# Moving the first branch into the last head of a delta rule: a hybrid decoder layer on one core

## The chip, the core and the metric

The kernel runs on one core of a Trainium2 chip. The metric is the device time of one execution in microseconds (us). The core has a tensor engine (PE, with its weight loads shown as PEld), a vector engine (DVE), a scalar engine (ACT), GpSimd (POOL) and SyncE (SP), which issues nearly all DMAs of this kernel. Each engine takes its instructions in the order in which the program lists them.

## The reference, cut to what matters

One decoder layer on 1024 tokens of width 1024, in float32: a half-weighted SwiGLU block, a mixer of two branches, a second SwiGLU block, and a final norm. The mixer:

```python
qa, ka, va, qkv_b, beta_raw, decay_raw, gdn_gate, gate_a, gate_b = jnp.split(h @ w_in, offsets, axis=-1)
# branch A: three groups of dilated windows, 4 heads of 64 each
for gi, (window, dilation) in enumerate(DSW_GROUPS):
    o, lse = dilated_window_attention(qa[:, :, sl], ka[:, :, sl], va[:, :, sl], window, dilation)
    outs.append(o)
    lses.append(lse)
wts = jax.nn.softmax(jnp.stack(lses, axis=0), axis=0)
ya = jnp.einsum('gbsh,gbshd->bshd', wts, jnp.stack(outs, axis=0))
# branch B: gated delta rule, 8 heads of 128
S_t = exp(g_t) * S_{t-1} (I - beta_t k_t k_t^T) + beta_t v_t k_t^T;  o_t = S_t q_t / sqrt(Dk)
ob = rmsnorm(ob, gdn_out_norm) * jax.nn.silu(gdn_gate)
merged = sigmoid(gate_a) * (ya @ w_branch_a) + sigmoid(gate_b) * (yb @ w_branch_b)
return merged @ w_out
```

## The kernel before, in words

**Arithmetic.** A float32 product is made of three matmuls of a reduced float32 type: each operand is split into a high part (a copy on ACT) and a low part (a subtraction on DVE). `split_to` (L165) does it for data, `ff_split` (L208) for weights, into rings of nine tiles `fH` and `fL`. A "wide" matmul streams 512 columns; the transposes and the delta rule's own products are "narrow" ones.

**Stages.** First SwiGLU with its down projection, attention of three groups (`attention_pair`), eight heads of the delta rule (`mixer`, L1260), the merge of the branches (`merge_out`, L1325), second SwiGLU with its down projection (`Down`, `ff_down`). The down projection is seven products of 11 pairs each, four PSUM banks at a time; with `outer=LAST` (4) the last product works its last four pairs bank by bank, so that each bank of a row can be finished while the others are still summed.

**The heads.** For each head, `gdn_keys` makes keys and queries with a short convolution (L950), the decay (L1001) and the matrices; `gdn_inverse` inverts a triangular matrix by 31 dependent steps on DVE (L1040 to L1046) and four groups of narrow matmuls (L1074 to L1096); `gdn_values` adds the values; `gdn_scan` (L1176) walks eight chunks: per chunk the narrow products L1191, L1195, L1199, L1204, L1211 with a DVE or ACT operation between each two. Head h+1 is prepared while head h is scanned. Between these narrow steps PE works on wide projections, among them 16 gate tiles (`gate_tile`), of which the last are kept for the last head.

**Combination of the groups.** `combine` (L903) loads, for each of eight row tiles, the three groups' outputs and maxima, forms their softmax weights (an exponential at L917, small DVE operations), the weighted sum (L926 to L929), two transposes (L932) and a store to the buffer `yad`. All eight tiles stand in head 0.

**The merge.** `merge_out` opens its own pool of on-chip memory, loads `yad` (L1336), splits it (`yaH`, `yaL`), multiplies it by `w_branch_a` in 96 wide matmuls and copies the results into `x2` (L1351). It loads the eight heads' results `ybd` and splits each into `hH` and `hL` (L1353 to L1355). Then come the second branch's products, the sigmoid gates (L1367) and the output product.

**What sets the order.** The program is traced once; a planner (`arrange`) takes it as a graph, gives every operation a price and a rank (the longest priced way to the end) and lists, engine by engine, the operation of highest rank that is ready; the program is then built a second time in that order. So one edit can move instructions far from it. Buffers' rings are fixed by the order of the source.

Of the kernel before, what the change touches and what calls it, by code (L numbers as in the profile page):

```python
# [15 lines left out]
P = 128  # L16
# [473 lines left out]
class Down:  # L490

    def __init__(self, C, wd):
        self.C = C
        self.wd = wd.rearrange("(p o k) n -> o k p n", o=2, k=P)
        self.lefts = {}
        self.raws = {}
        self.home = {}
        self.quarters = {}
        self.ops = []

    def left(self, n, p, tag="e"):
        if (n, p) not in self.lefts:
# [69 lines left out]
    def operands(self, n, p):  # L572
        C = self.C
        v = self.left(n, p)
        h = C.wp.tile([P, 512], F32R, name="fH", tag="fH", bufs=9)
        C.nc.scalar.copy(h, v.bitcast(F32))  # L576
        C.nc.vector.tensor_tensor(out=v, in0=v.bitcast(F32), in1=h.bitcast(F32), op=ALU.subtract)  # L577
        return (h, v), self.right(n, p)
# [29 lines left out]
def ff_down(C, x_dram, D_, done, mid=None):  # L608

    nc = C.nc  # L610
    acc = [None] * NT

    def part(t, n):
        if acc[t] is None:
            acc[t] = row(C, C.fx, "acc", None, None)
        return acc[t][:, n * 512:n * 512 + 512]

    def add(out, ps, base):
        nc.vector.scalar_tensor_tensor(out, ps, 0.5, base, op0=ALU.mult, op1=ALU.add)

    def e1(j, ps):
        nc.scalar.mul(part(j, 1), ps, 0.5)

    def e2(j, ps):
        add(part(j, 0), ps, part(j, 1))

    def e6(j, ps):
        add(part(j, 1), ps, part(j, 1))

    def e7(j, ps):  # L630
        add(part(4 + j, 0), ps, part(j, 1))

    def e5(j, ps):
        add(part(4 + j, 1), ps, part(4 + j, 0))
        add(part(j, 1), ps, part(j, 1))

    def residual(t):
        xt = row(C, C.fx, "xt", None, None)
        nc.sync.dma_start(xt, x_dram[t * P:t * P + P])
        nc.vector.tensor_tensor(out=acc[t], in0=acc[t], in1=xt, op=ALU.add)  # L640

    def e3(j, ps):
        add(part(j, 1), ps, part(j, 1))
# [12 lines left out]
    def side(p):
        if p < NT:
            residual(p)
        D_.last_sums(p)

    D_.product(0, e1, side=homes)
    D_.product(1, e2)
    D_.product(2, e6)
    D_.product(3, e7)
    D_.product(4, e5)
    D_.product(5, e3, side=side)
    D_.product(6, e4, LAST, mid)


def consts(C, I):  # L670
# [229 lines left out]
            nc.sync.dma_start(dst, o)  # L900


def combine(C):  # L903

    nc = C.nc
    for t in range(NT):
        oc = C.ms.tile([P, 792], F32, name="oc", tag="xs", bufs=2).rearrange("p (g q f) -> p g q f", g=3, q=2)
        for g in range(3):
            nc.sync.dma_start(oc[:, g], C.od[g][t * P:t * P + P])
# [266 lines left out]
def gdn_scan(C, X):  # L1176
# [6 lines left out]
    with band(C, f"h{h}"):  # L1183
# [45 lines left out]
        for q in range(2):  # L1229
# [2 lines left out]
                nc.tensor.transpose(ps[:, c * P:c * P + P], o[:, q * 4 + c, :], C.ident)  # L1232
            sl = slice(q * 512, q * 512 + 512)
            nc.vector.scalar_tensor_tensor(X.g[:, sl], ps, C.gon, X.g[:, sl], op0=ALU.mult, op1=ALU.mult)
        nc.sync.dma_start(C.ybd[h], X.g)


def gdn_consts(C, I):
# [21 lines left out]
def mixer(C, tc, I):  # L1260
# [9 lines left out]
    def fill(n):  # L1270
        for _ in range(n):
            if gates:
                gate_tile(C, w_in, *gates.pop(0))
# [8 lines left out]
    with tc.tile_pool(name="mx", bufs=1, reuse_waits="tile") as C.mx:  # L1282
# [17 lines left out]
                    n += 1  # L1300
        with tc.tile_pool(name="gd", bufs=1, reuse_waits="tile") as C.gd:
            X = gdn_keys(C, w_in, 0, decay(0))
            with band(C, "att"):
                combine(C)
            gdn_inverse(C, X)
            gdn_values(C, w_in, X)
            for h in range(HEADS):
                Y = None
                if h < HEADS - 1:
                    Y = gdn_keys(C, w_in, h + 1, decay(h + 1, FILL[1][h]))  # L1310
                gdn_gate(C, w_in, X)
                if h == HEADS - 1:
                    fill(len(gates))
                gdn_scan(C, X)
                if Y is not None:
                    gdn_inverse(C, Y)
                    gdn_values(C, w_in, Y)
                X = Y
# [6 lines left out]
def merge_out(C, tc, I, gB2):  # L1325
# [4 lines left out]
    def load(name):  # L1330
        return C.fx.tile([P, T], F32, name=name, tag="ld", bufs=2)

    ya = {}
    for a in (0, 1):
        v = load("yal").rearrange("p (k t) -> p k t", k=2)
        nc.sync.dma_start(v, C.yad[:, :, a * 512:a * 512 + 512])  # L1336
        for k in range(2):
            ya[k, a] = ff_e(C, "yaH", F32R), ff_e(C, "yaL", F32R)
            split_to(C, *ya[k, a], v[:, k])
    x2 = [row(C, C.fx, "x2", None, None) for _ in range(NT)]  # L1340

    def branch_a(f, a):
        return x2[a * 4 + f // 2][:, f % 2 * 512:f % 2 * 512 + 512]

    for f in range(8):
        if f % 4 == 0:
            W = load_w(C, (lambda r: r[:, :T].rearrange("p (k n) -> p k n", k=2),
                           I["w_branch_a"][:, f * P:f * P + 512].rearrange("(k p) n -> p k n", p=P)))
        for a in (0, 1):
            pa = proj(C, lambda k: [v[:, f % 4 * P:f % 4 * P + P] for v in W[k]], a, "tC" if a else "mm", 2, [ya[0, a], ya[1, a]])  # L1350
            nc.scalar.copy(branch_a(f, a), pa)  # L1351
        yb = row(C, C.fx, "ybl", None, None)
        nc.sync.dma_start(yb, C.ybd[f])  # L1353
        for ts in (slice(0, 512), slice(512, 1024)):
            split_to(C, C.hH[:, f, ts], C.hL[:, f, ts], yb[:, ts])  # L1355
    del ya, v, yb, W
    for a in (0, 1):
        ts = slice(a * 512, a * 512 + 512)
        m = []
        for f in range(8):  # L1360
# [5 lines left out]
            nc.sync.dma_start(sg[:, 1], C.sgbd[f][:, ts])  # L1366
            nc.scalar.activation(sg, sg, AF.Sigmoid)  # L1367
            pb = proj(C, lambda k: [v[:, k % 4 * P:k % 4 * P + P] for v in halves[k // 4]], a, "tC" if f % 2 else "mm")
            nc.vector.tensor_tensor(out=sg[:, 0], in0=sg[:, 0], in1=branch_a(f, a), op=ALU.mult)
            nc.vector.tensor_tensor(out=sg[:, 1], in0=sg[:, 1], in1=pb, op=ALU.mult)  # L1370
            nc.vector.tensor_tensor(out=sg[:, 0], in0=sg[:, 0], in1=sg[:, 1], op=ALU.add)
            m.append((ff_e(C, "mH", F32R), ff_e(C, "mL", F32R, "s3" if f > 4 else "e")))
# [33 lines left out]
def open_pools(C, tc, st):  # L1406
# [25 lines left out]
def layer(tc, I, out):  # L1432
# [6 lines left out]
    with ExitStack() as st:  # L1439
# [84 lines left out]
class Program:  # L1524
# [149 lines left out]
    def cost(self, k):  # L1674
# [13 lines left out]
            n *= c  # L1688
        q = self.queue[k]
        if q == 0:  # L1690
            t = {"R": n / 2.4 + 13, "T": 109, "F": 223, "S": n * 0.83 + 106, "s": n * 0.83 + 106, "Q": 117 if n > 32 else 63}[self.kind[k]]
            return t, t + 190
        ps = any(self.place[a["memref"]][0] == "PSUM" for a in aps)
        if q == 1:
# [191 lines left out]
```

## Time and profile before

| what | value |
|---|---|
| time, median of 3 runs (lowest to highest) | 2556.34 us (2556.09 to 2561.18) |
| the profiled execution | 2554.51 us |
| its span, first to last instruction | 2552.8 us |
| mean granted clock of PE | 0.994 |
| DVE, ACT busy | 1766.6, 974.1 us |

The span holds: the first SwiGLU with its projections to about 700 us, the attention to about 990, the heads to about 1690, the merge and the second SwiGLU after that. In the rows of a timeline the columns are start, duration (us), engine, line, operation, output <- inputs, shapes and a count; in brackets stands the idle time of the engine before it, and what ended it. In the rows of groups, the busy time and the mean length in ns stand behind the count, then the idle time ahead of the group.

### The profile page before, as it was taken

The numbers are of one execution on the slowest core, as the hardware profiler recorded it, in microseconds if no ns is written. First come the engines' busy times: TensorE is split into PE (matmuls) and PEld (weight loads), VectorE is DVE, ScalarE is ACT, GpSimd is POOL, SyncE is SP. The second block draws the span as 40 slices with busy tenths as digits, with TensorE's granted clock in tenths as the row PEclk, the third lists the DMA queues.
The fourth block names the chain that finished last, engine by engine and source line by source line (L and its number), as shares of the span: only waits on it lengthen the run. The fifth ranks groups of instructions, "written<-read, shape, count | busy, mean of one in ns | idle before, by whom it ended". The sixth has DMA issues, their size and how long they took to land.

```text
span 2552.8 us, 34782 instructions
## 1 busy us (share of the span) xinstructions
PE 2490.4 (98%) x12739; PEld 2070.5 (81%) x12739; DVE 1766.6 (69%) x4035; ACT 974.1 (38%) x1875; POOL 24.6 (1%) x36
## 2 busy tenths in 40 slices
PE   7999999999999999899999999989999999999997
PEld 7888888888988888678887887868888888888886
DVE  7866666768744455988878778345768666667588
ACT  4432232444423345542444334154443332223444
POOL 0000000000000000000000000000000000000000
PEclk9999999999999999999999999999999999999999
DMA  4233224836253322322121122165542223238453
GB/s 162 84 107 119 94 101 169 288 112 219 96 138 92 92 82 80 95 57 56 55 67 53 54 57 80 55 202 189 193 138 83 92 98 120 91 118 303 137 170 119
DMA packets 257786, 301.04 MB, mean 118 GB/s; under 512 B 41456, under 2 KB 174800, under 8 KB 257616
## 3 DMA queue, kind: packets, MB, share of 16 engines
q1 hardware_dynamic: 255312, 292.53, 34.8%
q10 hardware_dynamic: 2304, 6.29, 1.1%
q8 instruction: 100, 1.64, 0.3%
q14 instruction: 70, 0.57, 0.1%
HBM read 217.34 MB, written 75.14 MB: 115 GB/s over the span
## 4 chain that ended last, share of the span: by engine, by line
PE 86%; DVE 9%; DMA 2%; ACT 1%; issue 1%; SPq 0%; DVEq 0%; ACTq 0%
PE mm L161 19%; PE tC L404 13%; PE mm L404 9%; PE tM L404 8%; PE mm L584 5%; PE tC L584 4%; PE tM L584 4%; PE tA L584 4%; PE tA L161 3%; PE mm L697 2%; PE mm L274 2%; PE tC L274 2%; PE mm L1387 2%; PE tC L1387 1%; PE tC L161 1%; PE tA L890 1%
## 5 line engine op out<-in xcount | busy, mean ns | idle before, releaser
L216 ACT CAST fH<-fraw 128x512 fp32r<-128x512 f32 x482 | 290.2, 619 | 597.8 <-PE tC L404 258.8
L217 DVE TENSOR_TENSOR fL<-fraw,fH 128x512 fp32r<-128x512 f32 x482 | 318.9, 685 | 158.9 <-ACT fH L216 142.7
L161 PE MATMUL mm<-hH,fH 128*128 128x512 f32 x896 | 359.3, 403 | 2.3 <-ACT xp L828 2.3
L161 PE MATMUL mm<-hL,fH 128*128 128x512 f32 x896 | 356.0, 398 | 0.0
L161 PE MATMUL mm<-hH,fL 128*128 128x512 f32 x896 | 353.9, 399 | 0.1
L161 PEld LDWEIGHTS mm<-hH,fH 128*128 128x128 f32 x896 | 169.1, 189 | 33.7 <-ACT xp L828 2.7
L161 PEld LDWEIGHTS mm<-hH,fL 128*128 128x128 f32 x896 | 168.9, 188 | 33.6 <-issue 1.0
L161 PEld LDWEIGHTS mm<-hL,fH 128*128 128x128 f32 x896 | 169.1, 189 | 29.9 <-issue 0.3
L404 PE MATMUL mm<-hH,fH 128*128 128x512 f32 x320 | 124.5, 389 | 0.0
L404 PE MATMUL mm<-hH,fL 128*128 128x512 f32 x320 | 123.7, 389 | 0.0
L404 PE MATMUL mm<-hL,fH 128*128 128x512 f32 x320 | 122.6, 389 | 0.0
L577 DVE TENSOR_TENSOR hid<-hid,fH 128x512 fp32r<-128x512 f32 x154 | 104.5, 684 | 9.9 <-ACT fH L576 9.9
L576 ACT CAST fH<-hid 128x512 fp32r<-128x512 f32 x154 | 94.9, 616 | 14.4 <-DMA hid<-hd1x 9.1
L969 DVE SCALAR_TENSOR_TENSOR ka<-xp,cw,ka 128x512 f32<-128x512 f32 x96 | 73.9, 781 | 19.6 <-ACT ka L967 19.0
L216 ACT CAST fH<-hH 128x512 fp32r<-128x512 f32 x68 | 42.3, 622 | 86.8 <-PE tC L584 36.0
L431 DVE TENSOR_TENSOR e<-tC,e 128x512 f32<-128x512 f32 x40 | 27.3, 686 | 66.9 <-PE tC L404 66.9
L404 PEld LDWEIGHTS mm<-hH,fL 128*128 128x128 f32 x320 | 60.1, 188 | 12.5
L404 PEld LDWEIGHTS mm<-hL,fH 128*128 128x128 f32 x320 | 60.1, 188 | 12.5
L404 PEld LDWEIGHTS mm<-hH,fH 128*128 128x128 f32 x320 | 60.1, 188 | 12.5
L584 PE MATMUL tC<-fH 128*128 128x512 f32 x176 | 68.6, 390 | 0.0
L584 PE MATMUL tC<-fL,fH 128*128 128x512 f32 x176 | 68.5, 389 | 0.0
L584 PE MATMUL mm<-fL,fH 128*128 128x512 f32 x176 | 68.4, 390 | 0.0
(402 smaller groups left out, 6111.3 us busy)
## 6 DMA issues: line engine op xcount, KB each, us to landing
fraw<-in_w_in_dram SPq DMA_DIRECT2D x66, 512.0 KB, 3.7
fraw<-in_ffn_w_gate_dram SPq DMA_DIRECT2D x22, 1024.0 KB, 5.2
fraw<-in_ffn_w_up_dram SPq DMA_DIRECT2D x22, 1024.0 KB, 7.3
hL<-in_ffn_w_down_dram SPq DMA_DIRECT2D x8, 1024.0 KB, 6.9
fraw<-in_ffn_w_down_dram SPq DMA_DIRECT2D x8, 1024.0 KB, 5.7
fraw<-in_w_branch_b_dram SPq DMA_DIRECT2D x8, 1024.0 KB, 5.1
fraw<-in_w_out_dram SPq DMA_DIRECT2D x8, 1024.0 KB, 5.3
vb<-xp ACTq DMA_DIRECT2D x48, 128.0 KB, 2.4
```

The lines of the kernel that those rows point to most:

```text
L161: nc.tensor.matmul(ps, w, x, start=k == 0 and i == 0, stop=k == kt - 1 and i == 2)
L216: nc.scalar.copy(h, src)
L217: nc.vector.tensor_tensor(out=l, in0=src, in1=h.bitcast(F32), op=ALU.subtract)
L274: nc.tensor.matmul(ps[:, n0:n0 + n], w, x[:, k, c], start=k == 0 and i == 0, stop=k == KT - 1 and i == 2)
L404: nc.tensor.matmul(ps, w, x, start=opens and k == 0 and q == 0, stop=k == 3 and q == 2, skip_group_check=True)
L431: tt(out=p1[i], in0=ps, in1=p1[i], op=ALU.add)
L576: C.nc.scalar.copy(h, v.bitcast(F32))
L577: C.nc.vector.tensor_tensor(out=v, in0=v.bitcast(F32), in1=h.bitcast(F32), op=ALU.subtract)
L584: self.C.nc.tensor.matmul(ps, x[:, m], w, start=p == 0 and i == 0, stop=p == NPAIR - 1 and i == 2)
L697: nc.tensor.matmul(ps[:, :n], h[:, k, b * P:b * P + P], W[k][w], start=k == 0 and i == 0, stop=k == KT - 1 and i == 2)
L969: nc.vector.scalar_tensor_tensor(o, x, w, o, op0=ALU.mult, op1=ALU.add)
L1387: nc.tensor.matmul(ps, mx[:, c], W[k][w], start=i == 0, stop=i == len(seq) - 1)
```

## The change

1. `combine` takes a list of tiles and is called after each head's scan: two tiles with heads 1 and 6, one with heads 2 to 5, none with head 0.
2. The first branch is computed by a new function `branch_a` in the last head, ahead of its scan: loads of `yad`, splits, 96 matmuls, copies, and eight stores to new buffers `pad`. It also loads the results of heads 0 to 6 and splits them into `hH`, `hL` (`keep_head`). The last head's result is split where it is made and not stored.
3. `merge_out` loads the first branch's product from `pad` into `x2` and starts with the second branch.
4. In the second down projection the last product works its last seven pairs bank by bank (`closing`), and the high parts of its last five pairs lie in the ring `hid`.
5. The planner's price for the narrowest matmuls (32 columns) goes from 63 to 32.

```diff
@@ Down.operands
+        if self.closing and n == 4 and p >= NPAIR - 5:
+            h = ff_e(C, "hid", F32R)
+        else:
+            h = C.wp.tile([P, 512], F32R, name="fH", tag="fH", bufs=9)
@@ ff_down
-    D_.product(6, e4, LAST, mid)
+    D_.product(6, e4, D_.closing or LAST, mid)
@@ combine
-def combine(C):
+def combine(C, ts):
...
-    for t in range(NT):
+    for t in ts:
@@ gdn_scan
-        nc.sync.dma_start(C.ybd[h], X.g)
+        if h < HEADS - 1:
+            nc.sync.dma_start(C.ybd[h], X.g)
+        else:
+            keep_head(C, h, X.g)
+
+def keep_head(C, h, y):
+    for ts in (slice(0, 512), slice(512, 1024)):
+        split_to(C, C.hH[:, h, ts], C.hL[:, h, ts], y[:, ts])
+
+def branch_a(C, w):
+    nc = C.nc
+    with band(C, "bulk"):
+        ya = []
+        for k in range(2):
+            v, H, L = t4(C, "xp")[:, :T], t4(C, "ka", F32R)[:, :T], t4(C, "ka", F32R)[:, :T]
+            nc.sync.dma_start(v, C.yad[:, k])
+            for ts in (slice(0, 512), slice(512, 1024)):
+                split_to(C, H[:, ts], L[:, ts], v[:, ts])
+            ya.append((H, L))
+        for f in range(0, 8, 2):
...
+            for a in (0, 1):
+                ts = slice(a * 512, a * 512 + 512)
+                out = t4(C, "xp")[:, :T]
+                for i in (0, 1):
+                    c = (f % 4 + i) * P
+                    ps = proj(C, lambda k: [v[:, c:c + P] for v in W[k]], a, "mm", 2, [(H[:, ts], L[:, ts]) for H, L in ya])
+                    nc.scalar.copy(out[:, i * 512:i * 512 + 512], ps)
+                nc.sync.dma_start(C.pad[a * 4 + f // 2], out)
+        for h in range(HEADS - 1):
+            y = C.ms.tile([P, T], F32, name="yb", tag="xs", bufs=2)
+            nc.sync.dma_start(y, C.ybd[h])
+            keep_head(C, h, y)
@@ mixer
-            with band(C, "att"):
-                combine(C)
...
                 if h == HEADS - 1:
                     fill(len(gates))
+                    branch_a(C, I["w_branch_a"])
                 gdn_scan(C, X)
+                combine(C, {0: (), 7: (), 1: (0, 1), 2: (2,), 3: (3,), 4: (4,), 5: (5,), 6: (6, 7)}[h])
@@ merge_out
+    for i in range(NT):
+        nc.sync.dma_start(x2[i], C.pad[i])
@@ Program.cost
-... "Q": 117 if n > 32 else 63}
+... "Q": 117 if n > 32 else 32}
```

What this moves is seen in the printed order of the engines. The first place is PE at the end of the mixer (`vb` is the last head's result, turned by the eight transposes; `ya` or `ka` the attention result; `hH`, `hL` the heads' results). Before:

```order
L161 MATMUL mm<-hL_5720,fH 128x512
L161 MATMUL mm<-hH_5718,fL 128x512
L1232 MATMUL tC<-ident,vb 128x128 x8
L161 MATMUL mm<-yaH,fH 128x512 x2
L161 MATMUL mm<-yaL,fH 128x512
L161 MATMUL mm<-yaH,fL 128x512
L161 MATMUL mm<-yaH,fH 128x512
L161 MATMUL mm<-yaL,fH 128x512
L161 MATMUL tC<-yaH,fH 128x512
L161 MATMUL mm<-yaH,fL 128x512
L161 MATMUL tC<-yaH,fH 128x512
```

And with the change, in the same place:

```order
L161 MATMUL mm<-ka,fH 128x512 x2
L161 MATMUL mm<-ka,fL 128x512
L1236 MATMUL tC<-ident,vb 128x128 x8
L161 MATMUL mm<-hH_5395,fH 128x512
L161 MATMUL mm<-hL_5397,fH 128x512
L161 MATMUL mm<-hH_5395,fL 128x512
L161 MATMUL mm<-hH_5395,fH 128x512
L161 MATMUL mm<-hL_5397,fH 128x512
L161 MATMUL mm<-hH_5395,fL 128x512
L161 MATMUL mm<-ka,fH 128x512 x2
L161 MATMUL mm<-ka,fL 128x512
L161 MATMUL tC<-hH_5395,fH 128x512
```

All but three of the 96 products of the attention result now stand ahead of the last transposes, and the second branch stands right behind them.

The second place is PE where head 1 is begun (`seg` is the decay's operand, `vT` the values of head 0, `ka` keys and queries, `cy` the combination's sum). Before:

```order
L161 MATMUL mm<-hH_5718,fL 128x512
L932 MATMUL tA<-ident,cy 128x128 x2
L1160 MATMUL tA<-ident,vT 128x128 x8
L1008 MATMUL tA<-seg,strictR 128x512 x3
L979 MATMUL tA<-ident,ka 128x128 x4
L1008 MATMUL tA<-seg,strictR 128x512
L979 MATMUL tA<-ident,ka 128x128 x12
L1135 MATMUL tA<-ka 128x128 x4
L161 MATMUL mm<-hH_5387,fH 128x512
```

With the change, the first part of the same work:

```order
L1164 MATMUL tA<-ident,vT 128x128 x8
L161 MATMUL mm<-hH_5396,fH 128x512
L161 MATMUL mm<-hL_5398,fH 128x512
L161 MATMUL mm<-hH_5396,fL 128x512
L161 MATMUL mm<-hL_5728,fH 128x512
L161 MATMUL mm<-hH_5726,fL 128x512
L161 MATMUL mm<-hH_5726,fH 128x512
L161 MATMUL mm<-hL_5728,fH 128x512
L161 MATMUL mm<-hH_5726,fL 128x512
L1012 MATMUL tA<-seg,strictR 128x512 x2
L161 MATMUL mm<-hH_5395,fH 128x512
```

The run of narrow work is broken up by wide matmuls (L161), and the combination's transposes are gone from it.

The third place is DVE at the end of the program, where the four last banks are added (`acc`), the rows' norms are formed by small operations (`rnv`, `rny`, `rnt`) and the rows are scaled (`y`). Before:

```order
L217 TENSOR_TENSOR fL<-hH_20976,fH 128x512
L619 SCALAR_TENSOR_TENSOR acc<-mm,acc 128x512 x2
L123 TENSOR_SCALAR rnv<-ssq 128x1
L125 TENSOR_SCALAR rny<-rnv 128x1
L126 ISA rny<-rny,magic 128x2
```

With the change, at the third and fourth bank:

```order
L1517 SCALAR_TENSOR_TENSOR y<-acc,rny,gB 128x512
L623 SCALAR_TENSOR_TENSOR acc<-tC,acc 128x512
L1517 SCALAR_TENSOR_TENSOR y<-acc,rny,gB 128x512
L123 TENSOR_SCALAR rnv<-ssq 128x1
L125 TENSOR_SCALAR rny<-rnv 128x1
L126 ISA rny<-rny,magic 128x2
L623 SCALAR_TENSOR_TENSOR acc<-tC,acc 128x512
L128 TENSOR_TENSOR rnt<-rny 128x1
```

Before, the first two banks were added together and all four rows' norms stood behind that; now the first two rows are finished ahead of the third bank, and the last addition stands inside the third row's norm.

More of the change, by code (lines that the diff above doesn't have):

```diff
@@ L499, in __init__ @@
         self.ops = []
+        self.closing = 0
     def left(self, n, p, tag="e"):
@@ L574, in operands @@
         v = self.left(n, p)
-        h = C.wp.tile([P, 512], F32R, name="fH", tag="fH", bufs=9)
+        if self.closing and n == 4 and p >= NPAIR - 5:
+            h = ff_e(C, "hid", F32R)
+        else:
+            h = C.wp.tile([P, 512], F32R, name="fH", tag="fH", bufs=9)
         C.nc.scalar.copy(h, v.bitcast(F32))
@@ L1234, in gdn_scan @@
             nc.vector.scalar_tensor_tensor(X.g[:, sl], ps, C.gon, X.g[:, sl], op0=ALU.mult, op1=ALU.mult)
-        nc.sync.dma_start(C.ybd[h], X.g)
+        if h < HEADS - 1:
[16 more added lines that the diff above has]
+        for f in range(0, 8, 2):
+            if f % 4 == 0:
+                W = load_w(C, (lambda r: r[:, :T].rearrange("p (k n) -> p k n", k=2),
+                               w[:, f * P:f * P + 512].rearrange("(k p) n -> p k n", p=P)))
+            for a in (0, 1):
[10 more added lines that the diff above has]
+            keep_head(C, h, y)
 def gdn_consts(C, I):
@@ L1331, in load @@
         return C.fx.tile([P, T], F32, name=name, tag="ld", bufs=2)
[L1333 to L1339, printed above, removed]
-    x2 = [row(C, C.fx, "x2", None, None) for _ in range(NT)]
[L1342 to L1356, printed above, removed]
+    x2 = [row(C, C.fx, "x2", None, None) for _ in range(NT)]
+    for i in range(NT):
+        nc.sync.dma_start(x2[i], C.pad[i])
     for a in (0, 1):
@@ L1368, in merge_out @@
             pb = proj(C, lambda k: [v[:, k % 4 * P:k % 4 * P + P] for v in halves[k // 4]], a, "tC" if f % 2 else "mm")
-            nc.vector.tensor_tensor(out=sg[:, 0], in0=sg[:, 0], in1=branch_a(f, a), op=ALU.mult)
+            nc.vector.tensor_tensor(out=sg[:, 0], in0=sg[:, 0], in1=x2[a * 4 + f // 2][:, f % 2 * 512:f % 2 * 512 + 512], op=ALU.mult)
             nc.vector.tensor_tensor(out=sg[:, 1], in0=sg[:, 1], in1=pb, op=ALU.mult)
@@ L1426, in open_pools @@
     C.sgbd = [C.dp.tile([P, T], F32, name=f"sgbd{f}") for f in range(8)]
+    C.pad = [C.dp.tile([P, D], F32, name=f"pad{i}") for i in range(NT)]
     C.ybd = [C.dp.tile([P, T], F32, name=f"ybd{f}") for f in range(8)]
@@ L1484, in layer @@
             down = Down(C, I["ffn2_w_down"])
+            down.closing = 7
             ff_hidden(C, I["ffn2_w_gate"], I["ffn2_w_up"], first, down.start, False)
@@ L1690, in cost @@
         if q == 0:
-            t = {"R": n / 2.4 + 13, "T": 109, "F": 223, "S": n * 0.83 + 106, "s": n * 0.83 + 106, "Q": 117 if n > 32 else 63}[self.kind[k]]
+            t = {"R": n / 2.4 + 13, "T": 109, "F": 223, "S": n * 0.83 + 106, "s": n * 0.83 + 106, "Q": 117 if n > 32 else 32}[self.kind[k]]
             return t, t + 190
```

## The prediction

> **What bounds the kernel now.** I read the page first (span, busy shares, chain), then windows of 100 us, then the waits and the timeline where the tensor engine (PE) is not full.
>
> ```profile
> span 2552.8 us, 34782 instructions
> ...
> PE 2490.4 (98%) x12739; PEld 2070.5 (81%) x12739; DVE 1766.6 (69%) x4035; ACT 974.1 (38%) x1875; POOL 24.6 (1%) x36
> ...
> PE 86%; DVE 9%; DMA 2%; ACT 1%; issue 1%; SPq 0%; DVEq 0%; ACTq 0%
> ```
>
> PE is busy for 2490.4 of 2552.8 us and makes up 86% of the chain that ended last. Only 62.4 us of the span are not PE work, so a change that leaves the matmuls as they are can win idle time of PE and time at a lowered clock, and nothing else. The printed order holds the same matmuls and transposes in both kernels, in other places, so I look for where the idle time lies.
>
> ```profile
> 1000.00:1100.00 100.00, 91.00 (x513) 71.08 (x513) 85.48 (x302) 49.86 (x90) 2.65 (x4) 0.95 0.35 93
> 1100.00:1200.00 100.00, 98.23 (x587) 81.16 (x587) 85.54 (x277) 38.33 (x75) 5.09 (x6) 1.00 0.18 49
> 1200.00:1300.00 100.00, 97.62 (x604) 81.15 (x604) 74.06 (x211) 35.13 (x67) 2.62 (x4) 1.00 0.18 48
> 1300.00:1400.00 100.00, 96.22 (x621) 78.71 (x620) 85.74 (x247) 45.60 (x86) 5.25 (x6) 1.00 0.24 68
> 1400.00:1500.00 100.00, 99.08 (x588) 82.45 (x587) 78.28 (x230) 39.03 (x75) 2.83 (x4) 1.00 0.23 64
> 1500.00:1600.00 100.00, 97.74 (x590) 80.56 (x589) 81.53 (x254) 39.30 (x77) 2.81 (x4) 1.00 0.22 63
> ...
> 1024.00:1059.00 35.00, 33.55 (x150) 26.68 (x149) 33.40 (x132) 22.16 (x36) 0.00 (x0) 1.00 0.45 127
> 1059.00:1075.00 16.00, 11.24 (x45) 7.86 (x44) 15.70 (x34) 11.00 (x18) 2.02 (x3) 0.68 0.16 32
> ```
>
> The columns after the length are busy us of PE, PE's weight loads, the vector engine (DVE), the scalar engine (ACT) and GpSimd, then the granted clock. The five windows from 1100 to 1600 us are the ordinary state of the heads: PE idle for 1.8, 2.4, 3.8, 0.9 and 2.3 us, 2.2 on average. The window before them loses 9.0 us, 4.8 of it between 1059 and 1075, where the clock is 0.68 as well, and DVE is busy for 33.4 of 35 us and 15.7 of 16 us: PE starves behind DVE there. That is the stretch of head 0 and of the combination.
>
> ```profile
> 1687.23 1.33 DVE g L1234 x2
> ...
> 1688.95 6.92 DMA yal<-yad
> ```
> ```profile
> PE mm L161 <- ACT yaH L166: 9.7, 1, 9.7
> PE mm L161 <- ACT x L1351: 0.6, 2, 0.4
> PE tC L161 <- ACT x L1351: 0.2, 1, 0.2
> ```
> ```profile
> 1685.92 1.03 PE L1232 MATMUL tC<-ident,vb 128*128 128x128 f32 x8
> 1696.63 1.22 PE L161 MATMUL mm<-yaH,fH 128*128 128x512 f32 x2 [9.67 <-ACT yaH L166]
> 1697.64 0.63 PE L161 MATMUL mm<-yaL,fH 128*128 128x512 f32 x1
> 1700.18 0.39 PE L161 MATMUL tC<-yaL,fH 128*128 128x512 f32 x1
> ```
>
> The three fences are the chain, PE's waits and PE's timeline around the end of the mixer. The last transposes end at 1686.95; the pool of the next stage opens; a load of the attention result takes 6.92 us; its split follows; PE stands for 9.67 us. It then comes back slow: a matmul lasts 0.63 us instead of 0.39.
>
> **The change, term by term.** Sums are made against the profiled run, 2554.51 us (span 2552.8 and 1.7 around it); the median of the three runs, 2556.34, is 1.8 above that, and I apply the same difference to it.
>
> *A, the end of the mixer.* The 96 matmuls of the first branch now stand between the scan steps of the last head, and behind the last transposes PE has the second branch, whose operands are split already for heads 0 to 6. So no load stands between. Removed are 9.67 us of idling, 1.5 us of slow matmuls (nine start between 1696.63 and 1700.18; at 0.226 us each, 235 in the 53 us of the full window quoted under C, they would have taken 2.0 of these 3.55 us) and the waits of 0.6 and 0.2 us on the copies of line 1351: 12.0 us. What is late next: head 7 is needed only in the last eighth of the depth, behind some 40 matmuls (9 us) in the new order, while its gating and split are four operations under 0.7 us each; the sigmoid of the first gates is needed when four PSUM banks of 24 matmuls each are full, 4 x 24 x 0.226 = 21.7 us after the start. I take back 1 us for a few scan steps that stand closer together than before (four wide matmuls, 0.9 us, between two dependent steps). A = -11.0; bounds -12 and -6, if half the gap is only moved.
>
> *B, head 0 without the combination.* The eight combinations' DVE work is in these rows, and the last is one of eight small groups of 1.2 to 1.4 us:
>
> ```profile
> L926 DVE TENSOR_TENSOR oc<-oc,ce 128x384 f32<-128x384 f32 x16 | 8.3, 553 | 0.0
> ...
> L928 DVE TENSOR_TENSOR cy<-oc 128x256 f32<-128x256 f32 x8 | 3.4, 420 | 0.0
> L929 DVE TENSOR_TENSOR cy<-cy,oc 128x256 f32<-128x256 f32 x8 | 3.3, 418 | 0.0
> ...
> L920 DVE TENSOR_TENSOR cM<-cM,cz 128x4 f32<-128x4 f32 x8 | 1.2, 156 | 0.0
> ```
>
> They sum to 8.3 + 3.4 + 3.3 + 8 x 1.3 = 25.4 us, all before 1062 us, ahead of the decay of head 1 in a full DVE. Without them DVE has that much slack in the same stretch, and the printed order shows the run of narrow work without any wide matmul between gone. From 1059 to 1075 PE idles 4.8 us and does 11.24 us of work at 0.68, which is up to 3.6 us more; 1024 to 1059 idles 1.45. With the whole window's 9.0 that is 12.6, less the ordinary 2.2: 10.4. I take B = -9.0, since the 3.6 is an upper value; bounds -11 and -5.
>
> *C, the tail.* DVE sets the end:
>
> ```profile
> 2538.95 0.39 PE L584 MATMUL tC<-fH,hid 128*128 128x512 f32 x1
> ```
> ```profile
> 2533.48 0.69 DVE L619 SCALAR_TENSOR_TENSOR acc<-mm,acc 128x512 f32<-128x512 f32 x1 [0.93 <-PE mm L584]
> ...
> 2539.42 0.68 DVE L619 SCALAR_TENSOR_TENSOR acc<-tC,acc 128x512 f32<-128x512 f32 x1
> ...
> 2547.87 0.16 DVE L129 SCALAR_TENSOR_TENSOR rnt<-rnt,rnv 128x1 f32<-128x1 f32 x1
> 2548.06 0.16 DVE L130 SCALAR_TENSOR_TENSOR rny<-rnt,rny 128x1 f32<-128x1 f32 x1
> 2548.26 1.42 DVE L1493 SCALAR_TENSOR_TENSOR y<-acc,rny,gB 128x512 f32<-128x512 f32 x2
> ```
> ```profile
> 2540.19 1.06 ACT L186 ACTIVATE sq<-acc 128x1024 f32<-128x1024 f32 x1 [1.26 <-DVE rnt L129]
> 2541.16 0.19 ACT L186 ACTIVATION_READ_ACCUMULATOR sq<-acc 128x1 f32 x1
> ```
> ```profile
> 2478.00:2531.00 53.00, 53.00 (x235) 43.67 (x233) 50.76 (x115) 25.43 (x45) 0.00 (x0) 1.00 0.37 127
> ```
>
> From the last addition at 2539.42 to the last output row's end at 2549.68 there are 10.3 us. A row costs DVE an addition (0.6), twelve small operations 0.19 apart (2.3) and two halves of 1.4 together: 4.3 us. Banks of four pairs end 12 x 0.226 = 2.7 us apart, so rows pile up; banks of seven end 21 x 0.226 = 4.7 us apart, so they need not. In the new order the last addition stands after three small operations of the third row: behind PE's end come 0.6, nine small (1.75), 1.4, twelve small (2.3) and 1.4, 7.5 us in all. C = -2.8. Bounds: the pile gone entirely, -4.7 (one row alone behind PE's end: 0.6, 1.25 for its square and its sum on ACT, 2.3 and 1.4); and 0, since DVE is busy for 50.76 of the 53 us before and must now have all operands ready about 5 us earlier, or PE waits for them.
>
> *D, what the spread costs.* One combination more per head (two in heads 1 and 6) adds 25.4 / 8 = 3.2 us to windows in which DVE is busy for 74 to 86 us of 100, so it stays under 92. It also adds six table loads to ACT, by the printed order 38 instead of 32.
>
> ```profile
> 1041.53 1.28 ACT L970 ACT_TABLE_LOAD   x1
> 1042.82 0.63 ACT L970 ACTIVATE ka<-ka 128x512 f32<-128x512 f32 x1
> ```
>
> A load takes 1.28 us and the next activation starts 0.01 behind it: 6 x 1.28 = 7.7 us of ACT, which is busy for 35 to 46 us of 100. The bounds of D are 0 (all in slack) and +10.9 (the work costs PE as much spread as in a lump). I take +2, near the first, because no window comes near the 95 to 98% of DVE at which the lump hurt. The Trainium skill (ScalarE: Activation LUTs, What ACT_TABLE_LOAD costs) speaks against this spreading: it counts a drain of about 1.38 us on top of 1283 ns for each switch and asks to group by table set. The trace agrees with the 1283 and shows no drain behind it. By that page of the Trainium skill the six loads would be an estimated 16 us of ACT instead of 7.7.
>
> *At nothing:* the copies, splits and matmuls of the first branch are the same in number. New are eight stores and eight loads of 512 KB for its product, less one store and one load for head 7: hidden under 80 us of the last head, and at the merge in place of the eight loads that stood there. SP issues 7 loads of earlier heads, 2 of the attention result and 8 stores more in the last head, at 0.3 to 0.5 us each. The planner's smaller price for the narrowest matmuls only reorders; I bound it by 1 us either way. The first 996 us keep their order on every engine.
>
> Sum: -11.0 - 9.0 - 2.8 + 2.0 = -20.8, so 2554.5 becomes 2533.7 and the median **2535.5**.
>
> **Rivals.**
> 1. *Spread, not gone.* DVE and ACT are short in every head instead of one; each of the six added switches holds up a copy out of PSUM that PE waits for, 6 x 1.28 = 7.7, with the 2 of D near its upper bound: 2543. For: the printed order has runs of five kinds of narrow work in heads 2 to 6. Against: such runs stand there before too. By the drain of the same page and section of the Trainium skill, 6 x 1.38 on top, it would be an estimated 2551.
> 2. *A new wait at the merge.* SP issues in order; the last store of the first branch stands ahead of the first gate loads, and six loads of 512 KB ahead of the third pair. If a pair comes later than the 21.7 us above, PE waits for PSUM. The eight loads of 512 KB that stood there before had this median from issue to landing:
>
> ```profile
> ybl<-ybd SPq DMA_DIRECT2D x8, 512.0 KB, 5.8
> ```
>
> Six of them overlapping as the old ones did would be over in some 12 us, which fits; six in full turns would take 35 us, which does not. With A at its upper bound of -6: 2540.5.
> 3. *Slower: the last scan becomes the bound.* All of this now stands in the queues of ACT and DVE among the steps of the last head's scan:
>
> ```profile
> L167 DVE TENSOR_TENSOR hL<-ybl,hH 128x512 fp32r<-128x512 f32 x16 | 10.0, 686 | 5.3 <-ACT hH L166 5.3
> ...
> L166 ACT ACTIVATE hH<-ybl 128x512 fp32r<-128x512 f32 x16 | 8.9, 654 | 0.0
> ...
> L1351 ACT COPY x<-tC 128x512 f32<-128x512 f32 x8 | 4.7, 599 | 1.6 <-PE tC L161 1.6
> L1351 ACT COPY x<-mm 128x512 f32<-128x512 f32 x8 | 4.5, 590 | 9.9 <-PE mm L161 9.9
> ```
>
> Were every one of them in front of a step that PE waits for, it would be 10.0 + 8.9 + 9.2 = 28 us; the order of PE is written out, so the 96 matmuls behind such a step would wait too: +28 - 21 = +7, 2563. It decides once over 21 of the 28 are exposed. Against: the order has 22 wide matmuls (5 us) to most chunks, and a chunk's three operations take about 1 us.
> 4. *The change does not do what it says:* excluded by the order.
>
> **How the numbers follow.** Forecast 0.62 (2530 to 2540), rival 1 0.17, rival 2 0.10, all three terms at their best end (-12 - 11 - 4.7 + 0, about 2528.6) 0.07, rival 3 0.04. The range takes the best sum with one us of order below it, 2527, and reaches past rival 1 to 2546. A measurement of this kernel tells about 0.2%, 5 us, from no change. Faster 0.90: all but rival 3 and the worst part of rival 1; same 0.06; slower 0.04.
>
> **What would show it.** A: PE busy through the end of the mixer, at clock 1.00, no wait on a load of the attention result. B: the stretch behind 1000 us at 97 to 99 like its neighbours. C: about 7.5 us from PE's end to the last output row. D: idle time of PE in the later windows near 2 per 100. I would be wrong if the scan's steps in the last head, or the gate loads behind it, show up as PE's longest waits.

## The result and the profile after

The changed kernel runs in 2532.82 us (median of 4 runs, 2532.18 to 2533.24), the kernel before beside it in 2556.88 (4 runs): a ratio of 0.9903, 95% interval 0.9888 to 0.9917, which is 24 us less. The forecast was 2535.5 in a range of 2527 to 2546. The profiled execution took 2533.24 us, 21.3 less than the profiled one of before. First the page (span, busy time, shares of the chain):

```profile
span 2531.4 us, 34786 instructions
...
PE 2488.5 (98%) x12739; PEld 2071.9 (82%) x12739; DVE 1766.7 (70%) x4035; ACT 983.8 (39%) x1881; POOL 26.5 (1%) x36
...
PE 84%; DVE 11%; DMA 2%; ACT 1%; issue 1%; SPq 0%; DVEq 0%; ACTq 0%
```

The same matmuls stand there; PE is idle for 42.9 us instead of 62.4. Next the windows, with the columns of before:

```profile
1000.00:1100.00 100.00, 98.28 (x576) 80.07 (x576) 81.16 (x257) 40.77 (x74) 4.07 (x4) 0.98 0.21 53
1100.00:1200.00 100.00, 97.12 (x574) 80.32 (x573) 84.39 (x268) 40.42 (x76) 4.29 (x6) 1.00 0.22 59
1200.00:1300.00 100.00, 97.12 (x624) 78.79 (x622) 79.71 (x222) 48.20 (x87) 4.91 (x6) 0.98 0.24 66
1300.00:1400.00 100.00, 96.28 (x589) 79.91 (x588) 82.38 (x262) 43.26 (x83) 3.48 (x4) 0.97 0.27 73
1400.00:1500.00 100.00, 98.05 (x575) 80.65 (x574) 85.05 (x265) 41.24 (x77) 2.92 (x4) 1.00 0.24 66
1500.00:1600.00 100.00, 98.91 (x598) 82.97 (x597) 79.16 (x255) 39.95 (x78) 3.46 (x4) 1.00 0.26 72
...
1600.00:1703.00 103.00, 102.79 (x575) 84.67 (x573) 45.77 (x102) 43.42 (x87) 0.00 (x0) 1.00 0.50 169
1703.00:1745.00 42.00, 42.00 (x187) 34.76 (x186) 27.11 (x43) 21.25 (x30) 0.00 (x0) 1.00 0.92 333
```

The stretch behind 1000 us idles 1.7 us instead of 9.0. The five windows behind it idle 12.5 us together instead of 11.1, two of them at a clock of 0.97 and 0.98. The last head and the merge, 1600 to 1745, idle 0.2. PE's timeline at the end of the mixer shows the seam:

```profile
1701.91 0.39 PE L161 MATMUL mm<-ka,fL 128*128 128x512 f32 x1
1702.14 1.03 PE L1236 MATMUL tC<-ident,vb 128*128 128x128 f32 x8
1702.94 0.47 PE L161 MATMUL mm<-hH,fH 128*128 128x512 f32 x1
1703.25 0.39 PE L161 MATMUL mm<-hL,fH 128*128 128x512 f32 x1
```

The last matmuls of the first branch, the mixer's last transposes and the first ones of the second branch follow one another without a gap, the wide ones at 0.39 to 0.47 us. SP's timeline and the rows of the gates show whether the merge waits:

```profile
1706.20 0.32 SPq L1273 DMA_DIRECT2D pad<-xp  x1
1706.61 0.38 SPq L1387 DMA_DIRECT2D sgl<-sgad  x1
...
1710.54 3.04 SPq L1377 DMA_DIRECT2D x<-pad  x5
```
```profile
L1389 ACT ACTIVATE sgl<-sgl x16: 1047/1061/1063, 1714.6 to 1836.2; 128x1024 f32<-128x1024 f32 x16
```

The gates are loaded only behind the last store of the first branch, as feared, and the first sigmoid runs at 1714.6, 11.7 us behind the branch's first matmul at 1702.94 and ahead of the 21.7 at which PSUM would be full. The tail (timeline of PE and DVE):

```profile
2520.52 0.39 PE L588 MATMUL tC<-fH,hid 128*128 128x512 f32 x1
```
```profile
2520.95 0.68 DVE L623 SCALAR_TENSOR_TENSOR acc<-tC,acc 128x512 f32<-128x512 f32 x1
2521.56 0.15 DVE L128 TENSOR_TENSOR rnt<-rny 128x1 f32<-128x1 f32 x1
...
2526.93 1.42 DVE L1517 SCALAR_TENSOR_TENSOR y<-acc,rny,gB 128x512 f32<-128x512 f32 x2
```

From PE's end, 2520.91, to the end of the last output row, 2528.35, there are 7.4 us. From PE's end to the end of the span it is 10.5 us; before, it was 2552.8 - 2539.34 = 13.5.

### The profile page after: what moved, and what is told of

The parts are those of the page before. It is cut to its first block, busy times and chain, and to the rows that moved or that the text cites. A ratio compares the mean times of both kernels' runs of the same rounds, so it can differ in the third digit from the quotient of the medians.

```text
span 2531.4 us, 34786 instructions
## 1 busy us (share of the span) xinstructions
PE 2488.5 (98%) x12739; PEld 2071.9 (82%) x12739; DVE 1766.7 (70%) x4035; ACT 983.8 (39%) x1881; POOL 26.5 (1%) x36
## 4 chain that ended last, share of the span: by engine, by line
PE 84%; DVE 11%; DMA 2%; ACT 1%; issue 1%; SPq 0%; DVEq 0%; ACTq 0%
PE mm L161 19%; PE tC L404 13%; PE mm L404 9%; PE tM L404 8%; PE mm L588 4%; PE tC L588 4%; PE tM L588 3%; PE tA L588 3%; PE tA L161 3%; PE mm L701 2%; PE mm L274 2%; PE tC L274 2%; DVE ka L973 2%; PE mm L1409 2%; PE tC L1409 1%; DVE fL L217 1%
## 5 line engine op out<-in xcount | busy, mean ns | idle before, releaser
L161 PE MATMUL mm<-hH,fH 128*128 128x512 f32 x896 | 360.3, 404 | 2.5 <-ACT xp L832 2.4
L161 PE MATMUL mm<-hL,fH 128*128 128x512 f32 x896 | 356.8, 399 | 0.0
L161 PE MATMUL mm<-hH,fL 128*128 128x512 f32 x896 | 353.9, 400 | 0.0
L161 PEld LDWEIGHTS mm<-hH,fH 128*128 128x128 f32 x896 | 170.1, 190 | 34.8 <-ACT xp L832 2.9
L161 PEld LDWEIGHTS mm<-hH,fL 128*128 128x128 f32 x896 | 169.6, 189 | 33.9 <-issue 1.0
L161 PEld LDWEIGHTS mm<-hL,fH 128*128 128x128 f32 x896 | 169.9, 190 | 30.5 <-issue 0.3
L580 ACT CAST fH<-hid 128x512 fp32r<-128x512 f32 x149 | 91.8, 616 | 14.6 <-PE tC L588 5.0
L404 PEld LDWEIGHTS mm<-hH,fH 128*128 128x128 f32 x320 | 60.1, 188 | 12.7 <-ACT e L408 0.3
L404 PEld LDWEIGHTS mm<-hH,fL 128*128 128x128 f32 x320 | 60.1, 188 | 12.5
L588 PE MATMUL mm<-fH,hid 128*128 128x512 f32 x186 | 70.3, 389 | 0.0
L588 PE MATMUL tC<-fH,hid 128*128 128x512 f32 x186 | 70.3, 389 | 0.0
L404 PEld LDWEIGHTS mm<-hL,fH 128*128 128x128 f32 x320 | 60.1, 188 | 12.5
L351 DVE TENSOR_TENSOR s<-fraw 128x512 f32<-128x512 f32 x40 | 27.5, 687 | 54.0 <-DMA fraw<-in_ffn_w_gate_dram 53.4
```

The source lines that it names most:

```text
L161: nc.tensor.matmul(ps, w, x, start=k == 0 and i == 0, stop=k == kt - 1 and i == 2)
L351: tt(out=s3[i], in0=a11, in1=a21, op=ALU.subtract)
L404: nc.tensor.matmul(ps, w, x, start=opens and k == 0 and q == 0, stop=k == 3 and q == 2, skip_group_check=True)
L588: self.C.nc.tensor.matmul(ps, x[:, m], w, start=p == 0 and i == 0, stop=p == NPAIR - 1 and i == 2)
```

## The experiments

For every kernel I worked out **lost time** of PE from its timeline: the length of a stretch less its matmuls at the distance at which they follow one another undisturbed (0.2265 us with 512 columns, 0.108 with 128, 0.084 for 64x64, 0.022 for 32x32; the last two are rough, and the same for every kernel). It counts idle time and slow clock together, and differences between kernels are good to about 1 us. An example: between 1000 and 1100 us the kernel before has 272, 145, 32 and 64 of these, which is about 81.3 us of work; lost are about 18.7. Medians and ratios (95% interval) are of each kernel's own job, a set of runs taken together on one chip, beside runs of the kernel before, 2554.2 to 2558.1 by job; "tail" is the span behind PE's end. The jobs are: the changed kernel; e1 to e4; c1 with e5 to e7; e9 to e11; e12. A difference across jobs can come out up to 4 us apart by medians and by ratios, so both are given where it matters.

| kernel | median | ratio to before | lost 1000-1100 | lost 1100-1600 | lost 1600-1950 | tail |
|---|---|---|---|---|---|---|
| before | 2556.88 | 1 | 18.7 | 32.4 | 17.3 | 13.5 |
| changed | 2532.82 | 0.9903 (0.9888-0.9917) | 6.8 | 36.4 | 4.9 | 10.5 |
| changed, again (c1) | 2532.42 | 0.9906 (0.9892-0.9921) | 6.5 | 36.2 | 5.3 | 10.5 |
| e1 closing with 4 | 2533.43 | 0.9914 (0.9901-0.9928) | 6.9 | 34.8 | 6.3 | 13.4 |
| e2 combinations in head 0 | 2541.61 | 0.9951 (0.9938-0.9963) | 22.1 | 31.9 | 4.1 | 10.6 |
| e3 branch behind the mixer | 2541.31 | 0.9953 (0.9939-0.9967) | 6.3 | 33.4 | 19.9 | 10.4 |
| e4 price 63 | 2534.47 | 0.9919 (0.9905-0.9932) | 6.5 | 39.5 | 5.2 | 10.5 |
| e5 = e2 without DVE work | 2527.66 | 0.9888 (0.9871-0.9904) | 5.7 | 32.5 | 6.0 | 10.5 |
| e6 = changed without DVE work | 2527.64 | 0.9887 (0.9872-0.9901) | 6.2 | 32.9 | 5.6 | 10.5 |
| e7 without exponential | 2533.51 | 0.9906 (0.9891-0.9921) | 6.8 | 37.4 | 5.0 | 10.5 |
| e9 products on GpSimd | 2544.01 | 0.9944 (0.9931-0.9958) | 6.7 | 49.1 | 5.5 | 10.6 |
| e10 combinations in the last head | 2527.12 | 0.9880 (0.9866-0.9893) | 7.2 | 29.4 | 7.0 | 10.6 |
| e11 before + branch alone | 2550.05 | 0.9968 (0.9955-0.9980) | 22.2 | 38.5 | 4.6 | 13.4 |
| e12 = e10 with price 63 | 2534.48 | 0.9914 (0.9897-0.9931) | 7.1 | 35.9 | 6.9 | 10.6 |

### c1: the changed kernel again

No edit.

> The changed kernel itself, without an edit, as the measure for the runs beside it and for the spread of its own runs: a ratio to the kernel before of 0.990, PE idle for under 0.5 us between 1600 and 1750 us, and 10.5 us from PE's end to the end of the span.

Its time, its tail and its idle time behind 1600 us are as expected but for 0.1 us of the last (0.6), and the ratio is 0.9906. The runs spread from 2531.92 to 2534.60, so differences of 2 us between jobs stay unsure; c1 is the measure for the others.

### e1: the tail undone

```
-            down.closing = 7
```

> The changed kernel with one part undone: the last product of the second down projection keeps its last 4 pairs per row of output for the end instead of 7. Theory (the tail is worth what the traces show, 13.5 us from the start of the last matmul's end to the end of the span before, 10.5 us after): 3.0 us slower than the changed kernel, about 2536, with some 13.4 us between PE's end and the end of the span. Rival (the shorter tail is paid for ahead of it, since operands must be ready earlier): within 1 us of the changed kernel, with PE ending 2 to 3 us earlier.

PE's last matmul, and the page's span:

```profile
2517.18 0.39 PE L588 MATMUL tC<-fH,hid 128*128 128x512 f32 x1
```
```profile
span 2531.0 us, 34796 instructions
```

From PE's end (2517.57) it is 13.4 us, as before the change; all kernels with 7 have 10.4 to 10.6. By its signs the rival came true all the same: the medians are 1 us apart (2.0 by the ratios to the kernel before), and PE ends 2.8 us earlier than in c1. But that lead does not come from the tail. The 5000th matmul, near 1000 us and far ahead of what the edit touches, starts at 995.2 us here and at 997.5 in c1; in c1 the clock falls to 0.50 for 3.4 us near 720, here it does not. From 1000 to 1950 us both lose the same (sums of the three columns: 48.0 and 48.0), and the last 3000 matmuls take 674.3 us here and 674.2 in c1. So nothing is paid ahead of the tail, and the term is 2.9 us; the medians are too coarse for it.

### e2: the combinations back in head 0

```
             X = gdn_keys(C, w_in, 0, decay(0))
+            with band(C, "att"):
+                combine(C, range(NT))
...
-                combine(C, {0: (), 7: (), 1: (0, 1), 2: (2,), 3: (3,), 4: (4,), 5: (5,), 6: (6, 7)}[h])
```

> The changed kernel with one part undone: all eight combinations back in head 0. Theory (the lump starves PE): between 1000 and 1100 us PE idles some 9 us again at a mean clock of about 0.95, the later heads lose 2 to 4 us less, table loads fall back by about six; 6 to 10 us slower than the changed kernel, 2539 to 2543. Rival (spread, not gone: what the lump cost is only moved): within 2 us of the changed kernel, about 2533 to 2535.

It is 9.2 us slower by the medians of the two jobs (11.5 by the ratios), and "spread, not gone" falls: the lump loses 15.6 us more than c1 in its stretch and only 4.3 less in the heads behind. The loss is made up otherwise than the theory said, though: between 1000 and 1100 us PE idles 6.8 us instead of 9, at a clock of 0.86 instead of 0.95. PE's timeline has the two longest waits, and two microseconds a row, the windows show what follows (PE's busy time first, the clock third from the end):

```profile
1060.98 0.41 PE L936 MATMUL tA<-ident,cy 128*128 128x128 f32 x2 [1.93 <-DVE cy L933]
...
1070.24 1.11 PE L983 MATMUL tA<-ident,ka 128*128 128x128 f32 x4 [2.25 <-ACT ka L974]
```

```profile
1060.00:1062.00 2.00, 0.95 (x7) 0.75 (x8) 2.00 (x7) 0.37 (x1) 0.00 (x0) 1.00 0.00 0
1062.00:1064.00 2.00, 2.00 (x6) 1.11 (x6) 2.00 (x4) 0.00 (x0) 0.00 (x0) 0.50 0.30 80
...
1076.00:1078.00 2.00, 2.00 (x35) 1.70 (x34) 0.73 (x2) 0.59 (x1) 0.00 (x0) 0.50 0.00 0
...
1086.00:1088.00 2.00, 2.00 (x8) 1.80 (x8) 1.02 (x4) 0.90 (x2) 0.00 (x0) 0.50 0.00 0
...
1090.00:1092.00 2.00, 2.00 (x14) 1.68 (x13) 1.32 (x8) 0.80 (x2) 0.00 (x0) 1.00 0.00 0
```

DVE is full; PE waits for the combination's sum from it, later for ACT, and the clock falls to 0.50 and stays there for 27 us, the last 17 of them with PE busy. In the kernel before it was low for only 10 us in this stretch (1064.8 to 1075.0): the lump that e2 prices is a worse one than that of before, 22.1 us of lost time against 18.7.

### e3: the branch back behind the mixer

```
-                    branch_a(C, I["w_branch_a"])
```

In its place stand the loads, splits and matmuls of the kernel before, in `merge_out`.

> The changed kernel with one part undone: the first branch and the splits of the heads stand behind the mixer again. Theory (the idle time at the end of the mixer is gone, not moved): PE idles about 9.7 us at the mixer's end again with a lowered clock behind it, 12 to 13 us slower than the changed kernel, about 2545. Rival (the matmuls among the steps of the last scan give half of it back there): 5 to 8 us slower, about 2539.

The wait is there again (PE's timeline):

```profile
1683.34 1.22 PE L161 MATMUL mm<-yaH,fH 128*128 128x512 f32 x2 [8.62 <-ACT yaH L166]
```

The stretch 1600 to 1950 loses 14.6 us more than c1, and the heads before it lose 3.0 less. The gap itself is gone for good in the changed kernel, but part of its worth is given back earlier. The median is 8.9 us slower than c1, between theory and rival; by the ratios it is 12.0, as the theory has it. Lost time, 14.6 - 3.0 = 11.6, is nearer to the latter.

### e11: the branch alone

The kernel before with `branch_a` and `keep_head` in the last head, and nothing else of the change.

> The kernel before with one part of the change alone: the first branch and the splits moved into the last head; the combinations stay in head 0, the last product closes with 4, the price is 63. Theory (the parts add up): 12 to 13 us faster than the kernel before, a ratio of 0.9950, with the loss between 1000 and 1100 us and the 13.5 us of the tail as before. Rival (half of the gap is only moved): 5 to 7 us faster, 0.9975.

It wins 7.0 us by the medians of its job (8 by the ratio). The mixer's end gains what it should (17.3 lost before, 4.6 now), but the heads lose 22.2 + 38.5 = 60.7 us instead of 51.1. So the rival's size came true, at another place than it said: not at the last scan but up to 600 us earlier. The windows of before and of e11 over the heads:

```profile
1000.00:1600.00 600.00, 579.90 (x3496) 475.12 (x3496) 490.63 (x1514) 247.26 (x469) 21.25 (x28) 0.99 0.23 64
```
```profile
1000.00:1600.00 600.00, 579.85 (x3448) 473.06 (x3449) 480.38 (x1467) 244.98 (x462) 21.19 (x28) 0.98 0.24 65
```

DVE and ACT have less to do there than before, and none of the branch's splits stands in this stretch, so it is not new work that crowds the heads. What differs is the order that the planner made from the new graph; PE gets 48 matmuls less done in the same time, and the clock in the lump is low for 27 us (1061 to 1088) instead of 10.

### e4 and e12: the planner's price

```
-"Q": 117 if n > 32 else 32
+"Q": 117 if n > 32 else 63
```

> The changed kernel with one part undone: the planner's price of the narrowest matmuls is 63 again. Theory (the price only reorders): within 1.5 us of the changed kernel, 2531.5 to 2534.5. Rival (the smaller price carries part of the gain in the heads): 3 to 5 us slower, 2536 to 2538, with the loss between 1000 and 1600 us.

> The kernel with all combinations in the last head, with the planner's price of the narrowest matmuls at 63 instead of 32. Theory (the smaller price is worth some 2 to 5 us in the heads, as the runs with the price at 63 let suppose): 2 to 5 us slower than with 32 (2527.1), 2529 to 2532, the loss between 1000 and 1600 us. Rival (the price only reorders, and the difference was chance): 2526 to 2528.5.

Alone, e4 would be unclear: 2.0 us slower than c1 by medians of two jobs (3.3 by the ratios), between the two answers by the first and inside the rival's by the second, with 3.3 us more lost in the heads. e12 settles that the price does something: 7.4 us slower than e10 (8.7 by the ratios), more than its theory allowed and outside the spread of both (2532.95 to 2536.71 against 2525.92 to 2528.99). The windows of e10 and of e12 over the heads:

```profile
1000.00:1600.00 600.00, 590.09 (x3560) 484.94 (x3559) 486.54 (x1473) 244.74 (x459) 22.76 (x28) 1.00 0.22 61
```
```profile
1000.00:1600.00 600.00, 585.07 (x3532) 480.65 (x3531) 479.48 (x1448) 239.27 (x454) 22.24 (x28) 1.00 0.22 61
```

PE idles 9.9 us with 32 and 14.9 with 63. The groups of the narrowest matmuls in e10, same stretch:

```profile
L1084 PE MATMUL tM<-W,U 32*32 32x32 f32 x224 | 6.5, 193 | 2.1 <-issue 1.3 <-DVE W L1080 0.7
L1078 PE MATMUL tM<-Tm,ka 32*32 32x32 f32 x224 | 5.3, 192 | 0.0
```

11.8 us of busy time for 448 of them is 26 ns each: the old price was over twice that, the new one is near. That a truer price makes better lists is the likely reason, but only the effect was measured.

### e5, e6 and e7: what of a combination costs

e5 and e6 take DVE's part out of `combine`, in the lump and in the changed kernel:

```
-        nc.vector.tensor_tensor(out=M, in0=m[:, 0:1], in1=m[:, 1:2], op=ALU.max)
...
-        nc.vector.tensor_tensor(out=yv, in0=yv, in1=oc[:, 2, :, 0:128], op=ALU.add)
+        nc.scalar.activation(e, m, AF.Exp, scale=0.0)
...
-            nc.tensor.transpose(ps[:, f * P:f * P + P], y[:, f * P:f * P + P], C.ident)
+            nc.tensor.transpose(ps[:, f * P:f * P + P], oc[:, 0, f, 0:128], C.ident)
```

e7 replaces the exponential:

```
-        nc.scalar.activation(e, e, AF.Exp, scale=0.125)
+        nc.scalar.copy(e, e)
```

> All eight combinations in head 0, but without their work on DVE: the weights, the products and the sums of the three groups are left out, one group's rows are transposed as they are, and the scalar engine's exponential runs on the maxima unscaled and unused; loads, transposes, copies and stores stay. Theory (25 us of DVE in head 0 hold up PE): against the lump with its DVE work (2541.6 in the runs before), 8 to 14 us faster, 2528 to 2534, and the clock between 1050 and 1100 us is 0.95 or more. Rival (loads, transposes and table switches of the lump hold up PE): within 4 us of the lump, 2538 to 2542, with a clock near 0.72 there again.

> The changed kernel with the same DVE work of the combinations left out, the combinations spread over heads 1 to 6, the exponential kept and with it the table loads. Theory (spread, the work lies in DVE's slack, and what the spread costs is the table loads): within 2 us of the changed kernel. Rival (the spread work still holds up PE): 3 to 6 us faster than the changed kernel, the gain between 1100 and 1600 us.

> The changed kernel with the exponential of the combinations replaced by a copy of the same size, so that their switches of the scalar engine's tables go, six loads or more; all DVE work stays. Theory (the table loads are the price of the spread): 2 to 5 us faster than the changed kernel, the gain between 1100 and 1600 us. Rival (the scalar engine has slack for them, DVE is the price): within 1.5 us of the changed kernel.

Without DVE's work it makes no difference where the combinations stand: 2527.66 and 2527.64. So their work on DVE costs 14.0 us in e2's lump (2541.6 to 2527.7; 16 by the ratios) and 4.8 spread (2532.4 to 2527.6), and it makes no difference that these runs can tell where their loads, transposes, copies and table switches stand. The edit takes two things away at once, DVE's time and the wait of PE's transposes for DVE's result (the 1.93 us in e2): no run separates them. Each edit also has the planner lay out the heads anew. e5's window of the 50 us in which the lump's clock was low:

```profile
1050.00:1100.00 50.00, 49.00 (x344) 39.52 (x343) 44.02 (x140) 19.69 (x41) 3.29 (x4) 1.00 0.20 51
```

And e2's:

```profile
1050.00:1100.00 50.00, 44.62 (x259) 35.21 (x258) 41.09 (x113) 20.96 (x39) 2.17 (x3) 0.73 0.13 32
```

PE waits for 1.0 us there at full clock, and for 5.4 at 0.73 with the work. In e7 the scalar engine loads its tables 26 times instead of 38, and the time stays (2533.5 against 2532.4): the loads were never the price of the spread. The theory that e6 tested, work in DVE's slack for nothing, falls; the rival stands.

### e9: DVE's products on GpSimd

```
-            nc.vector.tensor_tensor(out=ov, in0=ov, ...
+            nc.gpsimd.tensor_tensor(out=ov, in0=ov, ...
```

and the two additions below it in the same way.

> The changed kernel with the products and the sums of the combinations (the two multiplications of 128x384 and the two additions of 128x256 per combination) on GpSimd instead of DVE. Theory (the spread combinations cost 4.8 us through DVE's time): these four groups are 15 of the 25.4 us of DVE, so some 3 us faster than the changed kernel, about 2529.5, if DVE's other work runs at its old pace. Rival (GpSimd's work slows DVE's, or its longer way holds up the last combinations): no faster or slower, 2532 to 2538, with longer DVE instructions beside it or a wait on the attention result.

It is 11.6 us slower than c1 (9.7 by the ratios). GpSimd's groups, and a wait of DVE between 1000 and 1650 us:

```profile
L930 POOL TENSOR_TENSOR oc<-oc,ce 128x384 f32<-128x384 f32 x16 | 17.5, 1113 | 108.4 <-DVE ce L926 64.8 <-DVE cM L923 18.7 <-DVE cl L1129 14.6
L1015 POOL TENSOR_SCALAR_AFFINE_SELECT Dm<-Dm 128x512 f32<-128x512 f32 x16 | 13.3, 831 | 181.9 <-ACT Dm L1014 155.5 <-DVE seg L999 26.4
```
```profile
DVE seg L999 <- POOL cy L933: 5.4, 4, 2.3
```

DVE's other instructions last as long as before (line 1142: 345 ns against 343), so it isn't slowed. GpSimd takes 1113 ns where DVE took 553, its queue also holds the masks of the decay (line 1015), and DVE stands for 5.4 us behind its sums: the decay's operand `seg` (line 999) shares its ring of two buffers with the combination's rows `oc`. That accounts for a part; where the rest of the 13 us lost between 1100 and 1600 goes was not traced.

### e10: the combinations in the last head

```
                     fill(len(gates))
+                    combine(C, range(NT))
                     branch_a(C, I["w_branch_a"])
```

> The changed kernel with all eight combinations in the last head, ahead of the first branch, where DVE is busy for 44 of 100 us. Theory (only DVE's fullness makes the combinations cost anything): the 4.8 us between 1000 and 1600 us go and little comes back, 3 to 5 us faster than the changed kernel, 2527.5 to 2529.5. Rival (the first branch waits for its operands and the wait at the end of the mixer comes back): 2533 to 2540, with PE idle for several us between 1600 and 1720 us.

2527.12 us, the fastest kernel of the study, 5.3 us below c1 and no slower than the kernels without the work. The heads lose 29.4 us instead of 36.2; from 1600 to 1950 it is 1.7 more, and the wait at the mixer's end does not come back. DVE's work is the same; it stands where DVE has room. That the room is the cause is not shown by this run alone, since the order of the heads is another one too: with the price at 63 the same move gains nothing by the medians (e12 2534.48, e4 2534.47), with 3.0 us less lost in the heads and 1.7 more behind.

## Why the prediction was right, point by point

The time is inside the range and 2.7 us below the forecast. By places the terms held: in the profiled runs the heads (1000 to 1600 us) lost 43.2 us instead of 51.1, which is -7.9 against B + D = -7; the end of the mixer 4.9 instead of 17.3, -12.4 against A = -11; the tail is -2.9 against -2.8. By causes they held less well. As steps from before, by the medians: branch alone -7.0 (e11), price about -5.6 (e11 to e2, -8.4, less the 2.8 of the tail), tail -2.8 or -2.9, spreading -9.2 (e2 to c1): -24.6 (a chain of steps that ends at c1, so this sum has to agree). In the heads the branch's new order cost 9.6 us of lost time, the price gave back 6.7 and the spreading 11.3: that these come to about the sum of B and D, which knew only the last of them, is luck.

- **A, the end of the mixer, -11.** The place was right: 12.7 us of lost time gone there in e11, and no wait behind it. The step that failed is "I take back 1 us for a few scan steps that stand closer together": what comes back is 9.6 us of lost time in e11 and 3.0 in the changed kernel (e3 against c1), and it comes back in the earlier heads, whose order the planner made anew.
- **"The planner's smaller price for the narrowest matmuls only reorders; I bound it by 1 us either way."** This is the step that was wrong. The price is worth 2.0 us (e4) and 7.4 (e12) by the medians. From e11 to e2 it is 5.6 by the medians, 1.4 by the ratios and 6.7 by the lost time of the heads, so most of what A's move did to the heads is repaired. With a program whose order is computed, "reorders" is no reason for nothing.
- **B, -9, and D, +2.** The mechanism was right: it is the combinations' work on DVE that starves PE in the lump (e5), and fewer table loads gain nothing (e7). Both sizes were low: e2's lump costs 14.0 us, the spread 4.8, the net -9.2 instead of -7. B was sized mostly from idle time, with 3.6 us at most for the clock; in e2 PE idles 5.5 us more between 1000 and 1100 us than in e5 and loses 16.4 more, so most of the price is the lowered clock. D leaned on "all in slack", but in heads where DVE is busy for about 80 of 100 us the work has a price. The 25.4 us are a sum of instructions' lengths, which overlap: without this work DVE's busy time falls by only 12.7 us (1766.9 in c1, 1754.2 in e6), and 4.8 us are over a third of that. The Trainium skill (ScalarE: Activation LUTs, Table sets: the hidden batching unit) asks to group by table set; here 12 loads fewer changed nothing, which fits ACT being busy for about 40 of 100 us.
- **C, the tail, -2.8.** Right: 2.9 to 3.0 by the profiles, and DVE's row behind PE's end has the order and the 7.4 us worked out (7.5).
- **The rivals.** No new wait at the merge: the first sigmoid was 10 us early. The last scan did not become the bound. "Spread, not gone" was true to 4.8 of the 14.0 us, but not through the table switches that it named (e7).

## What to carry to other kernels

Work of an engine that is not the bound has a price that depends on where it stands: look for the stretch where that engine is half idle and try it there, rather than spreading it evenly (e10 against the changed kernel, 5 us; with the price at 63 there was nothing to gain, e12 against e4). Where a planner writes the order, moving one piece re-lays everything, so measure each part alone and with the others, and hold the planner's prices against the trace. A stall of the tensor engine among short matmuls is to be priced with the clock behind it, not by its idle time.

## What the runs showed of the hardware that was not expected

In e2, PE waited for 2.0 us in all between 1058 and 1062, no more than 1.93 at a stretch, and for 3.3 more until 1072; the granted clock fell to 0.50 at 1062 and stayed there for 27 us, although PE was busy without a break from 1072 on. At the distances of the lost time the matmuls of these last 17 us need some 9, so the low clock costs about 8 us there. In the kernel before, a wait of 9.67 us was followed by only some 3 us of slow matmuls (1696.63 to 1699.6), all of 512 columns. The Trainium skill (TensorE: Matmul & The Clock Gate, Part 1) has the clock return after about 3.4 us of sustained activity: the second case agrees, the first does not. That the many narrow matmuls there keep the clock down is a guess. What fits it: the clock came back 3.2 us behind the last matmuls of 64x64 in e2 (1086.1, 1089.3) and 3.35 us behind them in e11 (1085.05, 1088.4), with 128x128 and 512-column matmuls in between, and the 10 us of low clock in the lump of the kernel before held no matmul of 32x32 or 64x64. No run here separates it.
